# Stages of a hybrid decoder layer placed by a build-time clock of the engines' queues, with 32-row tiles for the sampled sequences

## The chip, the cores and the metric

The kernel runs on one core of one Trainium2 chip. The metric is the device time in microseconds of one execution of the whole program. A smaller number is better.

## What is computed

One decoder layer is applied to 1024 prompt tokens and to 8 sampled sequences of 8 new tokens each, 1088 tokens in all, with a model width of 1024:

```
x <- LN1(alpha*x + 0.5*SwiGLU_1(x))
x <- LN2(alpha*x + W_out[ attention group | HGRN2 group ](x))
x <- LN3(alpha*x + 0.5*SwiGLU_2(x))

attention: 8 heads of 64, 2 key/value heads, window 128, ALiBi, sinks
HGRN2, 4 heads, keys 128, values 128, per chunk of the sequence:
  b = cumsum(log f)
  o = (q*exp(b)) @ S + tril(sum_k q k exp(b_t - b_s)) @ v
  S = exp(b_last)*S + (k*exp(b_last - b))^T @ v
then rms norm of o, times silu(gate)
```

The prompt starts HGRN2 with S = 0. Each sampled sequence starts with a state of its own, S0, and its state after 8 tokens is an output. The feed-forward width is 2816, which is 22 blocks of 128 features.

## The kernel before

The whole layer is one straight program for five engines. TensorE multiplies, VectorE (DVE) and ScalarE (ACT) evaluate, GpSimd (POOL) helps, and SyncE (SP) issues the transfers. The order on each engine is the order in which the Python code emits instructions, and every engine runs its own list in that order. So an instruction whose operand is late holds up all that stands behind it on its engine.

Precision sets the form of the large products. A weight tile (`raw`) is split into a rounded part and a remainder (`hl`: one ACT cast, one DVE subtraction, in `hilo`), and so are the activations; each product is then three passes (`mmr`). The products inside attention and HGRN2 are single fp32 matmuls (`mm`), which the trace shows as two records each.

The stages of the program are, in order of time:

- **Gate and up of the first FFN** (0 to about 470 us): five feature blocks in plain form, the others with seven half-size products (`u`, `y`, `z`) from sums of operands. The results `go` are spilled to HBM as `gd`.
- **Down projection of the first FFN** (about 470 to 780 us): the tokens are cut into three groups `CH` of 512, 288 and 288 (ci 0, 1, 2). `g` features are read back and split (`g_item`). `trio(ci, ahead)` makes three output rows at once, feature by feature, with the first `ahead` features already there; `whole(m, cis, more)` makes one output row `m` and carries loads `more` for later units. When a group's last row is done, its layer norm `ln_T` starts: transposes `nat`, statistics, `rsqrt` on POOL, then `Y<-Y,rb` products on DVE.
- **Mixer** (about 780 to 1290 us): 22 projections of `W_in` (`pp`), and between their matmuls the attention blocks (`attn_block` 0 to 7), the sampled attention (`attn_sample`) and the HGRN2 heads (`hgrn` 0 to 3). Then `W_out` in two halves, `wout_a` from attention and `wout_b` from HGRN2 (`py`).
- **The second FFN** (about 1290 us to the end), like the first, with eight plain blocks, and with the last norm (`ln_out`, `ln_tail`) going out.

The work between the matmuls is written as Python generators, called sides. A side emits one stage and then yields a number of nanoseconds. `poll`, called after every group of large matmuls, runs the next stage of each side whose time has come. The clock for this is `s.t`, which counts planned TensorE time alone:

```python
def stage(s, d):
    lat = next(d.gen, "end")
    ...
        d.ready = s.t + (lat or 0.0)
```

So how far apart two stages stand is a constant in the code (`yield 1800.0` after each of the seven levels of `hgrn`, `yield 2500.0` behind an `rsqrt`), and the clock knows nothing of the queues of DVE, ACT, POOL or SP. Each fp32 matmul with its default `cols=1` is booked with at least 222 ns.

In `hgrn`, a level of the prompt multiplies 32-row tiles (`hgrn_b`, results to four 32-partition strips of one PSUM bank). The 64 sampled tokens have one 64-row product per level in a bank of their own (`hgrn_c`, and the second `hgrn_a`). Their output takes eight products with the states S0 (`hgrn_f`, 8 columns each), a copy `it`, and two products in `hgrn_g`. Their new states take two 512-column products (`hgrn_i`) over `Ve`, which spreads the values of 64 tokens over 8 sequences with the mask `em`.

Of the kernel before, what the change touches and what calls it, by code (L numbers as in the profile page):

```python
# [55 lines left out]
def const_arrays():  # L56
# [24 lines left out]
    em=np.zeros((64,8),np.float32)  # L81
    em[np.arange(64),np.arange(64)//8]=1
# [53 lines left out]
class Ker:  # L136
    def __init__(s, tc):
        s.tc = tc
        s.nc = tc.nc
# [46 lines left out]
    def pt(s, b):  # L186
        return s.pm.tile([P, 512], F32, tag="pm", name=s.nm(b))

    def st(s, b):
        return s.ps.tile([P, 512], F32, tag="ps", name=s.nm(b))  # L190

    def t2(s, b, w=512):
        return s.tmp.tile([P, 576], F32, tag="t2", name=s.nm(b))[:, :w]
# [4 lines left out]

    def mm(s, out, lhsT, rhs, start, stop, cols=1):
# [3 lines left out]
        s.nc.tensor.matmul(out, lhsT, rhs, start=start, stop=stop, skip_group_check=cols > 1)  # L203

    def mmr(s, out, lhsT, rhs, start, stop, loose=False):
        s.t += out.free_size() / 2.4 + 12.5
        s.nc.tensor.matmul(out, lhsT, rhs, start=start, stop=stop, skip_group_check=loose)  # L207

    def tr(s, out, in_, ident):
        s.t += 109.0  # L210
        s.nc.tensor.transpose(out, in_, ident)  # L211
# [12 lines left out]
    def add(s, gen, delay=0.0, rank=1):  # L224
        d = Side(gen, s.t + delay, rank)
        s.sides.append(d)
# [3 lines left out]
    def stage(s, d):  # L230
# [4 lines left out]
        else:  # L235
            d.ready = s.t + (lat or 0.0)

    def poll(s, most=3):
# [3 lines left out]
        for d in list(s.sides):  # L242
            if most and d.ready <= s.t:
# [7 lines left out]
    def until(s, true):  # L251
        while not true():
            r = [x for x in s.sides if x.ready <= s.t]
            if not r:
                s.t = min(x.ready for x in s.sides)
# [29 lines left out]
    def room(s, n):  # L285

        while s.live + n > NROWS:
# [5 lines left out]
            r = [x for x in s.sides if x.ready <= s.t] or [min(s.sides, key=lambda x: x.ready)]  # L293
            s.t = max(s.t, r[0].ready)
# [245 lines left out]
    def consts(s, a):  # L540
# [7 lines left out]
        s.em = s.cst.tile([64, 8], F32, name="em")  # L548
# [357 lines left out]
    def ffn_units(s, w13, w2, w2t, res, ln, nd, ready=None, tail=None):  # L906
# [269 lines left out]
        def whole(m, cis, more=(), bank=None, steps=None, drop=None, end=None):  # L1176
# [5 lines left out]
            for i, (j, nb) in enumerate(CUTS):  # L1182
                at.append(len(items))
                items.append(s.piece(w2t[m, :, j : j + nb], nb))
                k = -(-len(more) // (len(CUTS) - i))
# [37 lines left out]
        def norm(ci):  # L1223
            return lambda: s.lns.append(s.add(ln(ci), 500.0))
# [792 lines left out]
```

## Time and profile before

| what | value |
|---|---|
| median of 3 runs | 2102.89 us (2102.34 to 2106.88) |
| profiled execution | 2100.44 us |
| span, first to last instruction | 2098.7 us |
| granted TensorE clock, mean | 0.996 |
| TensorE busy | 2050.0 us, 98% |
| VectorE busy | 1214.9 us, 58% |
| ScalarE busy | 834.5 us, 40% |
| GpSimd busy | 178.3 us, 8% |

The profile is of one execution, and its times are those of that execution. A matmul's span reaches past the start of the next one, because matmuls are pipelined; so TensorE counts as idle only where it waits longer than that overlap. A group's busy time in the view by line is the time covered by its spans, so groups that alternate cover some of the same time. "Idle before" is the wait in front of a group and the instruction that ended it.

### The profile page before, as it was taken

The page shows a single profiled execution, that of the slowest core. Times are in us where ns is not written, and L with a number is a line of the kernel's source. Part 1 is how long each engine was busy: PE and PEld are TensorE (multiplying, and loading weights), DVE is VectorE, ACT ScalarE, POOL GpSimd, SP SyncE. Part 2 cuts the span into 40 slices and gives each one's busy share as a digit, 9 for nine tenths or more (in the row PEclk, how much of TensorE's full clock was granted, in tenths as well). Part 3 has the DMA queues.
Part 4 walks back from the last instruction along what each step waited for, and adds up shares of the span by engine and source line. Part 5 has one row for each costly group of instructions (what it writes and reads, how often), then busy time and mean ns, then how long its engine had stood idle before and what let it go on. Part 6 is the DMA issues. An engine that isn't in the chain of part 4 may idle for free.

```text
span 2098.7 us, 40231 instructions
## 1 busy us (share of the span) xinstructions
PE 2050.0 (98%) x16089; PEld 1933.8 (92%) x16089; DVE 1214.9 (58%) x2463; ACT 834.5 (40%) x1886; POOL 178.3 (8%) x353
## 2 busy tenths in 40 slices
PE   8999999999999999999999999999999999999998
PEld 8999999998899999878888888998999999888997
DVE  7766555555357552465644767576666655444855
ACT  5443333334336443444443233454343333432521
POOL 0000000000020210022213201300000000000121
PEclk9999999999999999999999999999999999999999
DMA  6332222227357331101111132342222222655832
GB/s 236 96 103 88 88 75 80 70 81 236 118 165 237 90 111 62 31 22 39 36 53 38 47 124 64 105 139 83 88 83 95 91 78 74 209 159 165 272 104 93
DMA packets 126124, 221.97 MB, mean 106 GB/s; under 512 B 14336, under 2 KB 44032, under 8 KB 125920
## 3 DMA queue, kind: packets, MB, share of 16 engines
q1 hardware_dynamic: 125936, 219.39, 33.0%
q8 instruction: 126, 2.06, 0.4%
q14 instruction: 62, 0.51, 0.1%
HBM read 181.69 MB, written 38.63 MB: 105 GB/s over the span
## 4 chain that ended last, share of the span: by engine, by line
PE 40%; DVE 6%; ACT 2%; issue 2%; DMA 1%; POOL 1%; DVEq 0%; SPq 0%; ACTq 0%; POOLq 0%
PE py L207 13%; PE u L207 7%; PE y L207 5%; PE pp L207 5%; PE pg L207 2%; PE pu L207 2%; DVE hl L409 2%; PE z L207 1%; ACT hl L408 1%; PE nat L211 1%; PE hgrn_b L203 1%; PE hgrn_e L203 0%; PE attn_block_c L203 0%; DMA raw<-in_w2tb 0%; ACT ev L918 0%
## 5 line engine op out<-in xcount | busy, mean ns | idle before, releaser
L207 PE MATMUL py<-g,hl 128*128 128x288 f32 (+3 forms) x3234 | 540.9, 327 | 6.8 <-DVE hl L409 4.6
L207 PEld LDWEIGHTS py<-g,hl 128*128 128x128 f32 x3234 | 487.4, 188 | 55.0 <-DVE hl L409 9.5
L409 DVE TENSOR_TENSOR hl<-raw,hl 128x512 fp32r<-128x512 f32 (+1 forms) x600 | 387.8, 659 | 224.4 <-ACT hl L408 222.5
L408 ACT CAST hl<-raw 128x512 fp32r<-128x512 f32 (+1 forms) x600 | 351.7, 593 | 404.9 <-PE py L207 187.0
L207 PE MATMUL u<-T,hl 128*128 128x288 f32 (+1 forms) x2700 | 365.3, 291 | 6.0 <-ACT ev L1049 5.0
L207 PEld LDWEIGHTS u<-T,hl 128*128 128x128 f32 x2700 | 349.9, 189 | 10.0 <-ACT ev L1049 7.9
L207 PE MATMUL pp<-Xh,hl 128*128 128x288 f32 (+1 forms) x1056 | 272.2, 335 | 0.0
L207 PEld LDWEIGHTS pp<-Xh,hl 128*128 128x128 f32 x1056 | 182.7, 189 | 19.9 <-issue 5.0
L207 PE MATMUL pp<-Xl,hl 128*128 128x288 f32 (+1 forms) x528 | 173.1, 328 | 0.0
L634 POOL TENSOR_SCALAR lnt<-lnr,lnp 128x1 f32<-128x1 f32 (+1 forms) x81 | 41.2, 508 | 1510.8 <-DVE lnr L630 843.0
L918 ACT ACTIVATE ev<-ev 128x288 f32<-128x288 f32 (+1 forms) x150 | 65.0, 434 | 258.3 <-DVE ev L1054 171.4
L207 PE MATMUL z<-B,hl 128*128 128x288 f32 (+1 forms) x900 | 121.8, 290 | 2.1 <-DVE ev L1054 2.1
L207 PE MATMUL y<-T,hl 128*128 128x288 f32 (+1 forms) x900 | 122.0, 290 | 0.6 <-DVE T L467 0.6
L207 PE MATMUL u<-B,hl 128*128 128x288 f32 (+1 forms) x900 | 121.7, 290 | 0.0
L207 PE MATMUL y<-B,hl 128*128 128x288 f32 (+1 forms) x900 | 121.7, 290 | 0.0
L207 PEld LDWEIGHTS z<-B,hl 128*128 128x128 f32 x900 | 117.0, 189 | 2.3 <-DVE ev L1054 2.3
L207 PEld LDWEIGHTS y<-T,hl 128*128 128x128 f32 x900 | 117.1, 189 | 0.8 <-DVE T L467 0.8
L207 PEld LDWEIGHTS y<-B,hl 128*128 128x128 f32 x900 | 117.0, 189 | 0.0
L207 PEld LDWEIGHTS u<-B,hl 128*128 128x128 f32 x900 | 117.0, 189 | 0.0
L207 PEld LDWEIGHTS pp<-Xl,hl 128*128 128x128 f32 x528 | 99.8, 189 | 6.2
L409 DVE TENSOR_TENSOR hl<-S,hl 128x512 fp32r<-128x512 f32 x88 | 60.9, 692 | 74.8 <-ACT hl L408 74.4
L207 PE MATMUL py<-oH,hl 128*128 128x288 f32 (+1 forms) x384 | 96.5, 332 | 1.4 <-DVE Y L1836 1.4
(273 smaller groups left out, 2404.8 us busy)
## 6 DMA issues: line engine op xcount, KB each, us to landing
raw<-in_w13b SPq DMA_DIRECT2D x120, 256.0 KB, 3.2
raw<-in_w13a SPq DMA_DIRECT2D x108, 256.0 KB, 3.2
raw<-in_w2ta SPq DMA_DIRECT2D x75, 256.0 KB, 3.6
raw<-in_w2tb SPq DMA_DIRECT2D x75, 256.0 KB, 3.5
gd<-go SPq DMA_DIRECT2D x44, 288.0 KB, 3.2
raw<-gd SPq DMA_DIRECT2D x88, 144.0 KB, 3.3
gd<-go SPq DMA_DIRECT2D x44, 256.0 KB, 3.5
raw<-gd SPq DMA_DIRECT2D x44, 256.0 KB, 4.5
```

The source lines that it names most:

```text
L203: s.nc.tensor.matmul(out, lhsT, rhs, start=start, stop=stop, skip_group_check=cols > 1)
L207: s.nc.tensor.matmul(out, lhsT, rhs, start=start, stop=stop, skip_group_check=loose)
L211: s.nc.tensor.transpose(out, in_, ident)
L408: lambda: nc.scalar.copy(hl[:, 0, :nb], src),
L409: lambda: nc.vector.tensor_tensor(hl[:, 1, :nb], src, hl[:, 0, :nb].bitcast(F32), ALU.subtract),
L634: e.tensor_scalar(t, r, r, hp, ALU.mult, ALU.mult)
L918: nc.scalar.activation(si, ps, AF.Silu)
```

## The change

The build now carries a clock of all queues. The four other engines are wrapped (`Watch`), and every instruction that is emitted is booked on its engine with a price from a table `COST`: it starts when its engine is free and its operands are written, plus 50 ns. Each tile remembers when it is written and last read. A DMA is booked on SP and on one bus. TensorE's clock `s.t` waits in the same way (`pe`).

A side may now yield tiles, and a count of PSUM banks, in place of a number. It is due when the clock says that these tiles are written, plus 100 ns, and that so many of the five `ps` banks come free. Most stages of `attn_block`, `attn_sample` and `hgrn` yield in that way. Matmuls in narrow tiles are booked with `cols=2` or `cols=4`, which changes their price in the clock and not the instruction.

For the sampled sequences in HGRN2, 64-row tiles become pairs of 32-row tiles in the banks of the prompt (`hgrn_a`, `hgrn_b`), and `hgrn_c` goes. `hgrn_f` and `it` go too: a block-diagonal copy of the queries, `qm`, goes straight against S0 in `hgrn_g`, which is now two strips of 32 rows with five products each. `hgrn_i` becomes eight products of 32 rows and 256 columns, into two banks in turn.

`trio(1, 12)` becomes `trio(1, 18)`: the last unit of group 0 carries ten features of group 1 where it carried four. The layer norms of groups 0 and 1 in both FFNs are "soft": `poll` passes them over while the clock has VectorE booked more than 800 ns ahead.

The rows below show three places, in the order in which the engine runs them. Lines L187, L334, L338 and L342 are the wrapper and the helpers `mm`, `mmr` and `tr` of the changed file.

First, TensorE in the mixer, at the transposes of attention block 0's output (`attn_block_e`) among the projections `pp`. Before:

```order
L207 MATMUL pp_9712<-Xh_7876,hl_9524 128x512
L211 MATMUL attn_block_e_9729<-ident,ao_9581 128x128 x4
L211 MATMUL attn_sample_c_9738<-ident,ss_9632 128x128
L211 MATMUL attn_sample_c_9738<-ident,ss_9632 64x128
L211 MATMUL attn_block_d_9745<-ident,as_9552 128x128 x4
L207 MATMUL pp_9712<-Xh_7877,hl_9577 128x512
```

And now:

```order
L338 MATMUL pp_9803<-Xh_8263,hl_9578 128x288
L342 MATMUL attn_block_e_9817<-ident,ao_9582 128x128 x4
L334 MATMUL attn_sample_a_9826<-cache_9178,sp_9789 32x64 x4
L334 MATMUL attn_sample_a_9826<-vs,sp_9789 32x64 x4
L342 MATMUL attn_block_d_9837<-ident,as_9549 128x128 x4
L334 MATMUL attn_block_c_9693<-vn_9114,pT_9797 128x64 x4
L338 MATMUL pp_9803<-Xh_8264,hl_9607 128x288
```

The block's transposes now come two half groups of projection matmuls later, and behind the sample's `attn_sample_c`, which they used to precede.

Second, TensorE at the sampled output of HGRN2 head 0, again among `pp`. Before, with the rows of two projection groups left out in the middle:

```order
L203 MATMUL hgrn_f_10910<-Q_9508,S_10799 128x8 x8
L207 MATMUL pp_10929<-Xh_7875,hl_10669 128x512
L207 MATMUL pp_10929<-Xl_7879,hl_10669 128x512
...
L207 MATMUL pp_10929<-Xh_7876,hl_10669 128x512
L203 MATMUL hgrn_g_10946<-Vs_9950,A_9968 64x128
L203 MATMUL hgrn_g_10946<-ident,it_10919 64x128
L207 MATMUL pp_10929<-Xh_7877,hl_10719 128x512
```

And now:

```order
L338 MATMUL pp_10740<-Xh_8264,hl_10389 128x288
L334 MATMUL hgrn_g_10790<-Vs_9950,A_9968 32x128 x2
L334 MATMUL hgrn_g_10790<-S_10718,qm 32x128 x8
L342 MATMUL attn_block_e_10805<-ident,ao_10590 128x128 x4
L338 MATMUL pp_10814<-Xh_8820,hl_10318 128x288
```

Two stages, of eight matmuls and of two, are now one stage of ten matmuls at one place in the list.

Third, VectorE in the first FFN's `trio` of group 1, while the norm of group 0 (`Y<-Y,rb`) is under way; `hl` of 384 columns is the weight remainder for one feature, `g` the split of a feature. Before:

```order
L409 TENSOR_TENSOR hl_6837<-raw_6658,hl_6837 128x384
L705 TENSOR_TENSOR Y_5825<-Y_5825,rb_6791 128x256
L706 TENSOR_TENSOR Y_5825<-Y_5825,rb_6791 128x256
L705 TENSOR_TENSOR Y_5825<-Y_5825,rb_6791 128x256
L706 TENSOR_TENSOR Y_5825<-Y_5825,rb_6791 128x256
L1117 TENSOR_TENSOR g_6851<-raw_6672,g_6851 128x288
L409 TENSOR_TENSOR hl_6853<-raw_6714,hl_6853 128x384
L1117 TENSOR_TENSOR g_6851<-raw_6728,g_6851 128x288
L409 TENSOR_TENSOR hl_6880<-raw_6773,hl_6880 128x384
```

And now:

```order
L187 TENSOR_TENSOR hl_6866<-raw_6687,hl_6866 128x384
L187 TENSOR_TENSOR Y_5827<-Y_5827,rb_6820 128x256 x4
L187 TENSOR_TENSOR hl_6880<-raw_6701,hl_6880 128x384
L187 TENSOR_TENSOR hl_6903<-raw_6743,hl_6903 128x384
L187 TENSOR_TENSOR Y_5828<-Y_5828,rb_6820 128x256 x4
L187 TENSOR_TENSOR hl_6917<-raw_6757,hl_6917 128x384
L187 TENSOR_TENSOR hl_6943<-raw_6802,hl_6943 128x384
```

Between two bursts of the norm there are now two weight tiles and no feature; the six features have moved into the unit before. The second half of that norm, four more bursts that used to follow within the next unit and a half, now comes two or three units later.

The diff, cut to what matters:

```diff
+class Clock:
+    HOP = 50.0
+    def there(s, ap):
+        lo, hi = s.span(ap)
+        return max((t for a, b, t in s.wrote.get(ap.name, ()) if a < hi and b > lo), default=0.0)
+    def soonest(s, tag, bufs, n=1):
+        q = s.tags.get(tag, [])
+        i = len(q) + n - 1 - bufs
+        return s.used.get(q[i], 0.0) if 0 <= i < len(q) else 0.0
+    def run(s, e, cost, outs, ins):
+        t = max([s.free[e]] + [s.there(x) + s.HOP for x in ins + outs]) + cost
+        s.free[e] = t
...
+COST = dict(
+    DVE=lambda op, n: 160.0 + 0.62 * n if op in ("tensor_scalar", "tensor_copy", "memset") else 150.0 + 1.05 * n,
+    ACT=lambda op, n: 195.0 + 0.78 * n,
+    POOL=lambda op, n: 100.0 + 0.85 * n if op == "memset" else 340.0 if n == 1 else 190.0 + 2.7 * n,
+)
...
+    def pe(s, out, lhsT, rhs, cost):
+        c = s.clock
+        t = max(s.t, c.there(lhsT) + c.HOP, c.there(rhs) + c.HOP, c.held.get(out.name, 0.0) + c.HOP)
+        s.wait(out, lhsT, rhs, t)
+        s.t = t + cost
...
     def mm(s, out, lhsT, rhs, start, stop, cols=1):
         n = out.free_size()
-        s.t += 2 * (max(111.0, n * (2 / 2.4) + 24.0) if cols == 1 else (n * (2 / 2.4) + 24.0) / cols)
+        s.pe(out, lhsT, rhs, 2 * (max(111.0, n * (2 / 2.4) + 24.0) if cols == 1 else (n * (2 / 2.4) + 24.0) / cols))
...
+    def due(s, d):
+        return max(d.ready, s.clock.soonest("ps", 5, d.banks) if d.banks else 0.0)
...
         for d in list(s.sides):
-            if most and d.ready <= s.t:
+            if most and s.due(d) <= s.t and not (d.soft and s.clock.free["DVE"] > s.t + 800.0):
...
-            return lambda: s.lns.append(s.add(ln(ci), 500.0))
+            return lambda: s.lns.append(s.add(ln(ci), 500.0, soft=ci < 2))
...
+            if last:
+                more = [g_items(1, *x) for x in ((8, 9), (9, 10), (10, 11), (11, 14), (14, 16), (16, 18))]
...
-        units.append(trio(1, 12))
+        units.append(trio(1, 18))
...  attn_block, behind the rsqrt and before the transposes
-        yield 2500.0
+        yield r
         nc.vector.tensor_scalar(o, o, r, None, ALU.mult)
-        yield 700.0
+        yield o, 1
...  hgrn, each level
-            if smp:
-                p2 = s.st("hgrn_c_")
-                s.mm(p2[:64, :32]..., KL[:, 1024:1088], v(QR[:, 1024:1088], 64, 1), True, True)
+            if smp:
+                for b in range(2):
+                    k0 = 1024 + 32 * b
+                    s.mm(ps[32 * b : 32 * b + 32, 128:144]..., KL[:, k0 : k0 + 32], v(QR[:, k0 : k0 + 32], 32, 1), True, True, cols=4)
...
-            yield 1800.0
+            yield KL, QR, 1
...  hgrn, sampled output
-        ps = s.st("hgrn_f_")
-        for b in range(8):
-            s.mm(ps[:, b * 8 : (b + 1) * 8], S0[:, b * P : (b + 1) * P], QR[:, 1024 + 8 * b : 1032 + 8 * b], True, True)
-        it = s.t2("it")
-        nc.scalar.copy(it[:, :64], ps[:, :64])
-        yield 500.0
+        nc.vector.tensor_copy(s.qm..., QR[:, 1024:1088]...)
+        yield s.qm, S0, 1
         ps = s.st("hgrn_g_")
-        s.mm(ps[:64, :P], A[:64, 1024:1088], Vs, True, False)
-        s.mm(ps[:64, :P], it[:, :64], s.ident, False, True)
+        for b in range(5):
+            for g in range(2):
+                out = ps[32 * g : 32 * g + 32, :P]
+                if b == 0:
+                    s.mm(out, A[:64, 1024 + 32 * g : 1056 + 32 * g], Vs, True, False, cols=2)
+                else:
+                    x = (4 * g + b - 1) * P
+                    s.mm(out, s.qm[:, g, 32 * b - 32 : 32 * b], S0[:, x : x + P], False, b == 4, cols=2)
...  hgrn, behind the rsqrt and before the transposes hgrn_h
-        yield 2800.0
+        yield r5
...
-        yield 2500.0
+        yield on, ons, 3
...  hgrn, new states
+        pss = [s.st("hgrn_i_") for q in range(2)]
+        for x in (slice(0, 256), slice(256, 512)):
+            for q in range(2):
+                r = slice(32 * q, 32 * q + 32)
+                s.mm(pss[q][:, x], Ks[r], Ve[r, x], True, True, cols=2)
         for q in range(2):
-            ps = s.st("hgrn_i_")
-            s.mm(ps, Ks, Ve[:64, q * 512 : (q + 1) * 512], True, True)
+            ps = pss[q]
```

More of the change, by code (lines that the diff above doesn't have):

```diff
@@ L92, with __init__, span, write @@
 NRAW = 7
+class Clock:
+    HOP = 50.0
+    def __init__(s):
+        s.free = dict(DVE=0.0, ACT=0.0, POOL=0.0, SP=0.0)
+        s.bus = 0.0
+        s.wrote = {}
+        s.used = {}
+        s.held = {}
+        s.tags = {}
+    @staticmethod
+    def span(ap):
+        p = ap.ap
+        st = abs(p[0][0])
+        if str(ap.space).endswith("DRAM"):
+            return ap.offset, ap.offset + sum(abs(a) * (b - 1) for a, b in p) + 1
+        o = ap.offset % st if st else ap.offset
+        return o, o + sum(abs(a) * (b - 1) for a, b in p[1:]) + 1
+    def there(s, ap):
+        lo, hi = s.span(ap)
+        return max((t for a, b, t in s.wrote.get(ap.name, ()) if a < hi and b > lo), default=0.0)
+    def write(s, ap, t):
+        lo, hi = s.span(ap)
+        s.wrote[ap.name] = [x for x in s.wrote.get(ap.name, ()) if x[0] < lo or x[1] > hi] + [(lo, hi, t)]
+        s.use(ap, t)
+    def use(s, ap, t):
+        s.used[ap.name] = max(s.used.get(ap.name, 0.0), t)
+    def fresh(s, ap, tag, bufs):
+        q = s.tags.setdefault(tag, [])
+        q.append(ap.name)
+        if len(q) > bufs:
+            t = s.used.get(q.pop(0), 0.0)
+            s.wrote[ap.name] = [(0, 1 << 30, t)]
+            s.held[ap.name] = t
+        return ap
+    def soonest(s, tag, bufs, n=1):
[5 more added lines that the diff above has]
+        s.free[e] = t
+        for x in ins:
+            s.use(x, t)
+        for x in outs:
+            s.write(x, t)
+        for x in ins + outs:
+            s.held[x.name] = t
+    def dma(s, out, in_):
+        t = max(s.free["SP"], s.there(in_) + s.HOP, s.there(out) + s.HOP) + 450.0
+        s.free["SP"] = t
+        n = 1
+        for a, b in out.ap:
+            n *= b
+        s.bus = max(s.bus, t + 800.0) + n * 4 / 330.0
+        s.use(in_, s.bus)
+        s.write(out, s.bus + 600.0)
@@ L95, with __init__ @@
+class Engines:
+    def __init__(s, clock, nc):
+        s.vector = Watch(clock, "DVE", nc.vector)
+        s.scalar = Watch(clock, "ACT", nc.scalar)
+        s.gpsimd = Watch(clock, "POOL", nc.gpsimd)
+        s.sync = Watch(clock, "SP", nc.sync)
+        s.tensor = nc.tensor
 class Side:
@@ L138, in __init__ @@
         s.tc = tc
-        s.nc = tc.nc
+        s.clock = Clock()
+        s.nc = Engines(s.clock, tc.nc)
         s.uid = 0
@@ L1513, in hgrn @@
         A = s.row(F32, "A")
-        yield 1000.0
-        nc.gpsimd.memset(A[:, :1024], 0.0)
-        D = s.mx.tile([P, 8, 32], F32, tag="D", name=s.nm("D"))
+        yield KL, QR, 1
+        nc.gpsimd.memset(A, 0.0)
+        D = s.mx.tile([P, 9, 32], F32, tag="D", name=s.nm("D"))
         ps = s.st("hgrn_a_")
```

177 lines of the change are left out of this document (116 added, 61 removed).

## The prediction

> **What bounds the kernel now.** I read the page first, for the busy shares, and then the table of stretches, since one share says nothing of where time can be had.
>
> ```profile
> span 2098.7 us, 40231 instructions
> PE 2050.0 (98%) x16089; PEld 1933.8 (92%) x16089; DVE 1214.9 (58%) x2463; ACT 834.5 (40%) x1886; POOL 178.3 (8%) x353
> ```
>
> TensorE (PE) is the bound, with 48.7 us idle in the whole span. So a change pays in two ways only: less TensorE work, or shorter waits of TensorE. Each row below is a stretch, its length, and the busy time of PE; the difference is TensorE's idle time.
>
> ```profile
> 600.00:700.00 100.00, 97.57 (x701) 93.71 (x700) 64.49 (x145) 50.02 (x107) 11.88 (x28) 1.00 0.60 186
> 850.00:1250.00 400.00, 387.45 (x4184) 338.08 (x4183) 239.60 (x569) 161.59 (x483) 89.02 (x148) 1.00 0.16 50
> 1290.00:1445.00 155.00, 145.25 (x1157) 142.55 (x1156) 113.73 (x221) 75.75 (x144) 16.78 (x42) 0.99 0.36 117
> 1925.00:1970.00 45.00, 41.26 (x297) 38.76 (x295) 38.72 (x86) 17.83 (x39) 11.99 (x24) 1.00 0.73 229
> 1970.00:2098.70 128.70, 117.67 (x905) 116.38 (x904) 71.27 (x144) 36.59 (x68) 19.91 (x37) 0.97 0.43 131
> ```
>
> That is 2.4 us at the first FFN's `trio` of group 1, 12.6 us in the mixer, 9.8 us at the second FFN's start, 3.7 us at its `trio`, and 11.0 us to the end. The granted clock is about 1.00 nearly everywhere, so nothing is to be had there. The view of TensorE's waits, taken by stretch (the first six rows are of the mixer), says who is late; its columns are the sum, the number and the longest.
>
> ```profile
> PE hgrn_b L203 <- POOL KL L1558: 3.1, 3, 1.9
> PE attn_block_e L211 <- DVE sden L1422: 1.8, 1, 1.8
> PE attn_sample_c L211 <- DVE ss L1425: 1.7, 1, 1.7
> PE hgrn_b L203 <- DVE Q L1557: 1.7, 2, 1.2
> PE attn_sample_d L203 <- ACT ssq L1463: 1.1, 1, 1.1
> PE nat_a L211 <- ACT V L1264: 1.1, 1, 1.1
> PE py L207 <- DVE hl L409: 1.9, 5, 0.7
> PE py L207 <- DVE hl L409: 2.1, 4, 1.0
> PE py L207 <- DVE g L1117: 1.5, 1, 1.5
> PE pg L207 <- ACT B L466: 2.7, 1, 2.7
> ```
>
> **Part 1, TensorE's work for the sampled sequences in HGRN2.** The view by line with shapes apart gives busy time and count of records, two for each emitted matmul:
>
> ```profile
> L203 PE MATMUL hgrn_f<-Q,S 128*128 128x8 f32 x64 | 7.4, 251 | 0.0
> L203 PE MATMUL hgrn_i<-KL,Ks 64*128 64x512 f32 x16 | 7.9, 615 | 0.0
> L203 PE MATMUL hgrn_g<-ident,it 128*64 128x128 f32 x8 | 1.7, 298 | 0.0
> L203 PE MATMUL hgrn_g<-Vs,A 64*64 64x128 f32 x8 | 1.7, 294 | 0.0
> L203 PE MATMUL hgrn_c<-Q,KL 128*64 128x32 f32 x24 | 3.6, 232 | 0.1
> L203 PE MATMUL hgrn_a<-Q,KL 128*64 128x64 f32 x8 | 1.3, 246 | 0.0
> L203 PE MATMUL hgrn_d<-Vn,F 128*128 128x128 f32 x64 | 8.5, 275 | 0.0
> L203 PE MATMUL attn_block_a<-kT,qT 64*128 64x256 f32 x56 | 16.0, 406 | 0.0
> L203 PE MATMUL hgrn_b<-Q,KL 128*32 128x16 f32 x1280 | 14.7, 185 | 4.8 <-POOL KL L1558 3.1 <-DVE Q L1557 1.7
> ```
>
> The first six rows go or change: 7.4 + 7.9 + 1.7 + 1.7 + 3.6 + 1.3 = 23.6 us. In their place come, for four heads: `hgrn_g` with 10 emitted matmuls of 128 columns each, 80 records in two column strips; `hgrn_i` with 4 of 256 columns, 32 records in two row strips; 24 more matmuls (48 records) in `hgrn_b` and 8 more (16 records) in `hgrn_a`. No row here shows these very tiles. If two strips run side by side, a pair costs what one record of a full tile does: 40 x 8.5/64 = 5.3 us for `hgrn_g`, and by the attention scores, whose row tiles a and b already run two at a time, 16 x 16.0/56 = 4.6 us for `hgrn_i`. The extra records cost, at the pace of `hgrn_b`, 64 x 14.7/1280 = 0.7 us. Sum 10.6 us, a saving of 13.0 us. If the strips run one after the other, it is 10.6 + 9.1 + 0.7 = 20.4 us, a saving of 3.2 us. I take 13.0: these pairs are nearest to two rows that overlap already. In `hgrn_b` four column strips start a record every 11.5 ns, though its mean record lasts 185 ns. The scores' row strips start together:
>
> ```profile
> 858.54 0.38 PE L203 MATMUL attn_block_a<-kT,qT 64*128 64x256 f32 x1
> 858.55 0.38 PE L203 MATMUL attn_block_b<-kT,qT 64*128 64x256 f32 x1
> 858.76 0.38 PE L203 MATMUL attn_block_a<-kT,qT 64*128 64x256 f32 x1
> ```
>
> A rule speaks against the column strips. The Trainium skill, "TensorE: Matmul & The Clock Gate", section "Part 3: Packing small matmuls — row/col tiling", says that a weight load runs under a matmul in flight only where the two use different row groups. By it `hgrn_g`, whose strips share all row groups, would gain nothing from pairing and cost 10.6 us, so that the saving would be 7.7 us. The pace of `hgrn_b`, whose strips share them too, does not bear that out.
>
> What else this part moves lies beside TensorE: per head one ACT copy (`it`) goes and two small ones come, one DVE copy (`qm`) comes, `Ve` on POOL halves. ACT is 40% busy in the mixer's stretch (161.59 of 400), DVE 60%, POOL 22%, so I cost that at nothing. The cover is that slack; gone, each late microsecond would show as a wait for A, `qm` or `Ve`.
>
> **Part 2, stages placed by the clock, in the mixer.** The waits behind a yield that now names its tiles are those of `hgrn_b`, `attn_block_e`, `attn_sample_c` and `attn_sample_d`: 3.1 + 1.7 + 1.8 + 1.7 + 1.1 = 9.4 us of the 12.6. The wait of `nat_a` and the rest stand outside it. An exact clock would remove 9.4 us; one that is no better than the constants would remove nothing. Two of its prices are low. It books the 13 small POOL instructions of a head's `rsqrt` at 13 x (190 + 2.7 x 9) = 2.8 us; the first and last of them in head 3, of 13 rows in the timeline, span 3.98 us:
>
> ```profile
> 1217.67 0.20 POOL L637 TENSOR_TENSOR hgt<-hgr 128x9 f32<-128x9 f32 x1 [6.27 <-DVE hgr L630]
> 1221.41 0.24 POOL L1652 TENSOR_SCALAR hr<-hgr 128x9 f32<-128x9 f32 x1
> ```
>
> So `hgrn_h`, which waits for nothing now, is placed 1.2 us early per head, 4.8 us for four. A stage can only stand between half groups of projections, which on average delays it by about as much, so I book half, 2.4 us. And it books VectorE's scaling of a block's output without regard to POOL:
>
> ```profile
> L1369 DVE TENSOR_SCALAR ao<-ao,atr x8: 478/483/1562, 874.5 to 1100.6; 128x512 f32<-128x512 f32 x8
> 874.40 0.95 POOL L1517 MEMSET A<- 128x1024 f32 x1
> 874.50 1.13 DVE L1369 TENSOR_SCALAR ao<-ao,atr 128x512 f32<-128x512 f32 x1
> 875.78 0.41 PE L211 MATMUL attn_block_e<-ident,ao 128*128 128x128 f32 x2 [1.85 <-DVE sden L1422]
> L1369 DVE TENSOR_SCALAR ao<-ao,atr 128x512 f32<-128x512 f32 x8 | 5.6, 698 | 4.5 <-POOL atr L635 4.5
> ```
>
> The minimum, median and maximum of eight are 478, 483 and 1562 ns; the 1.13 us one ran under a POOL memset, and TensorE stood 1.85 us behind it. The mean is 698 ns, so 8 x 0.215 = 1.7 us stays. The Trainium skill, "Advanced Engine Details and Errata", section "VectorE Performance Modes", says that VectorE's second SBUF port is shared with GpSimd and that the two block each other; the trace agrees. The part gives 9.4 - 2.4 - 1.7 = 5.3 us.
>
> **Part 3, ten features early and soft norms.** While group 0's norm runs, two features cost DVE one burst and two splits and two weight remainders:
>
> ```profile
> 644.37 0.41 DVE L705 TENSOR_TENSOR Y<-Y,rb 128x256 f32<-128x256 f32 x1
> 645.94 0.45 DVE L1117 TENSOR_TENSOR g<-raw,g 128x288 fp32r<-128x288 f32 x1
> 646.30 0.68 DVE L409 TENSOR_TENSOR hl<-raw,hl 128x512 fp32r<-128x512 f32 x1
> L207 PE MATMUL py<-g,hl 128*128 128x288 f32 x2046 | 285.4, 297 | 6.7 <-DVE hl L409 4.6 <-DVE g L1117 1.5
> ```
>
> From start to start a burst takes 1.57 us and a split 0.36; a 384-column remainder lies between that and the 0.60 of 512 columns, say 0.5. That is 1.57 + 0.72 + 1.0 = 3.3 us, against 18 matmuls of 285.4/2046 us, 2.5 us, on TensorE. DVE falls behind by 0.8 us per burst. Without the two splits it needs 2.6 us and keeps up. The features go to a unit of 512-column matmuls, and the late half of the norm to units behind; over the whole 600 to 700 stretch DVE is 64% busy, which is the cover. Moving six `gd` reads ahead leaves SP's number of transfers as it is. The two stretches hold 2.4 + 3.7 = 6.2 us idle; I take three quarters, 4.6, since DVE is 86% busy in the second (38.72 of 45) and the norm's work stays. If the soft norm slips too far, what is late next is group 1's input of the first projection.
>
> **Part 4, nothing.** The start of the second FFN (9.8 us, with 2.7 of it for `B`) keeps its order of norm, sums and plain blocks, and the tail (11.0 us) its own. No gain, no loss; either could be 2 us.
>
> **The sum.** 13.0 + 5.3 + 4.6 = 22.9 us off the profiled execution's 2100.4 us gives 2077.5 us. That execution stands 2.5 us under the median of its runs, 2102.9; so 2080 us.
>
> **Rivals.**
> - *The waits only change places* (2090). For it: TensorE waits 48.7 us of 2098.7 already, every stage moved, and the prices above are low. Against: the present constants ignore the queues. Then part 1 alone stays, 2102.9 - 13.0 = 2090.
> - *The strips run in turn* (2090). Part 1 gives 3.2, the others 9.9: 2102.9 - 13.1 = 2090. By the skill's rule alone, 7.7 + 9.9 off, 2085. Against both stands `hgrn_b`'s pace.
> - *The clock runs ahead of the chip, and TensorE waits at each stage* (slower). The clock books a pair of scores at 2 x 2 x (256 x 2/2.4 + 24) = 0.95 us; the rows at 858 us show 0.21 per pair of records, so 0.42. A score stage of two pairs puts the clock 1.06 us ahead, and what is placed next comes too early by up to that. Six places in each of eight blocks, 48, could pay it. It decides at 13.0 + 4.6 + 12.6 = 30 us, 28 places; at all 48, 50.9 us, the time is 2102.9 - 30.2 + 50.9 = 2124. Against: work placed well behind a score is due by later writes, which move with the clock.
> - *No change that can be measured*: 20 such places take back 21 of the 22.9 us, 2101.
>
> **How the numbers follow.** The forecast has a chance of 0.57, its own range 2070 to 2087. The waits changing places has 0.15, the strips in turn 0.11 (0.03 of it by the skill's rule), no change 0.09, slower 0.08. 0.2% is 4.2 us, about what a measurement of this kernel can tell from no change. Faster is 0.57 + 0.15 + 0.11 = 0.83. The low end takes 13.0, all of 12.6 and of 6.2, and 2 at the second FFN: 33.8 off, 2069; I go to 2067. The high end takes in the two rivals at 2090 and some new waits, 2096.
>
> **What would show it.** Right: `hgrn_f` and `hgrn_c` gone, `hgrn_g` near 5 us, `hgrn_i` near 5; under 8 us idle in the mixer, no waits of `py` for `hl` over 1 us at the `trio`. Wrong: `hgrn_g` near 11, new waits in front of `hgrn_h` or `attn_block_d`, or a gap at group 1's first projection.

## The result, and the profile after

The changed kernel takes 2075.0 us (median of four executions, 2073.2 to 2076.4) against 2104.3 (2102.3 to 2106.9): a ratio of 0.9862, interval 0.9849 to 0.9874, 29 us less. The forecast was 2080 us, its own range 2070 to 2087. The profiled execution took 2073.2 us, 27.2 less than that of before. The page's first lines:

```profile
span 2071.5 us, 40371 instructions
PE 2029.2 (98%) x16137; PEld 1922.3 (93%) x16137; DVE 1213.9 (59%) x2467; ACT 834.2 (40%) x1890; POOL 180.9 (9%) x354
```

TensorE's busy time fell by 20.8 us and its idle time by 6.4, to 42.3. The groups of HGRN2's sampled tiles, by line with shapes apart:

```profile
L334 PE MATMUL hgrn_b<-Q,KL 128*32 128x16 f32 x1328 | 15.1, 185 | 2.2 <-POOL KL L187 1.9 <-DVE Q L187 0.3
L334 PE MATMUL hgrn_i<-KL,Ks 32*128 32x256 f32 x32 | 4.5, 400 | 0.0
L334 PE MATMUL hgrn_g<-S,qm 128*32 128x128 f32 x64 | 4.3, 276 | 0.0
L334 PE MATMUL hgrn_g<-Vs,A 64*32 64x128 f32 x16 | 1.6, 281 | 0.0
```

`hgrn_f` and `hgrn_c` are gone; 5.9 + 4.5 us and half a microsecond of extra records stand where 23.6 stood, 12.7 us less. From the view of TensorE's waits over the whole span, rows that bear on the prediction (sum, number, longest):

```profile
PE pg L338 <- ACT B L187: 8.5, 2, 5.8
PE py L338 <- DVE hl L187: 3.9, 6, 1.5
PE pu L338 <- ACT si L187: 2.2, 1, 2.2
PE hgrn_b L334 <- POOL KL L187: 1.9, 2, 1.2
PE attn_block_b L334 <- ACT sp L187: 0.9, 1, 0.9
```

The waits of `attn_block_e`, `attn_sample_c` and `attn_sample_d` are gone, nothing waits in front of `hgrn_h`; the wait of `pu` for `si`, at 24.6 us, is new. To see where the time went I cut both traces at the same instructions (the first `trio` matmul, the first attention score, the first `w_out` matmul and so on) and compare the stretches. Each row is start and end, length, TensorE's busy time, then its clock and two columns on DMA. By such cuts the stages of the kernel before begin at 485.7 us (down projection), 761.6 (mixer) and 1300.1 (second FFN), some 10 to 20 us off the round times of the list of stages. First the three of before, then of after: group 1's `trio` and the rest of the down projection, attention and HGRN2, and the same as the first for the second FFN.

```profile
608.00:761.60 153.60, 151.17 (x1127) 1.00 0.54 162
835.20:1178.10 342.90, 334.29 (x3729) 1.00 0.12 39
1926.90:2074.90 148.00, 143.69 (x1072) 1.00 0.57 176
```

```profile
609.20:758.50 149.30, 148.90 (x1127) 1.00 0.53 162
832.10:1157.50 325.40, 322.71 (x3773) 1.00 0.13 41
1902.10:2047.70 145.60, 141.71 (x1072) 1.00 0.55 173
```

The mixer's stretch is 17.5 us shorter, the two `trio` stretches 4.3 and 2.4. Of the rest, from the same cuts: -3.3 from `w_out` to the second FFN, -1.0 at that FFN's start, +1.2 in all that lies ahead of the first `trio`, the tail the same. From 850 to 1250 us TensorE is now idle for 6.3 us instead of 12.6.

### The profile page after: what moved, and what is told of

It reads as the page before. It is cut to its first block, busy times and chain, and to the rows that moved or that the text cites. A ratio compares the mean times of both kernels' runs of the same rounds, so it can differ in the third digit from the quotient of the medians.

```text
span 2071.5 us, 40371 instructions
## 1 busy us (share of the span) xinstructions
PE 2029.2 (98%) x16137; PEld 1922.3 (93%) x16137; DVE 1213.9 (59%) x2467; ACT 834.2 (40%) x1890; POOL 180.9 (9%) x354
## 4 chain that ended last, share of the span: by engine, by line
PE 40%; DVE 6%; DMA 2%; ACT 2%; issue 1%; POOL 0%; DVEq 0%; SPq 0%; ACTq 0%; POOLq 0%
PE py L338 13%; PE u L338 7%; PE y L338 5%; PE pp L338 5%; PE pu L338 2%; PE pg L338 2%; DVE hl L187 2%; PE z L338 1%; ACT hl L187 1%; DMA raw<-in_w2tb 1%; DVE ev L187 1%; DVE Y L187 1%; DVE S L187 1%; ACT ev L187 1%; PE nat L342 1%
## 5 line engine op out<-in xcount | busy, mean ns | idle before, releaser
L338 PE MATMUL py<-g,hl 128*128 128x288 f32 (+3 forms) x3234 | 536.7, 326 | 4.4 <-DVE hl L187 3.9
L338 PEld LDWEIGHTS py<-g,hl 128*128 128x128 f32 x3234 | 486.9, 188 | 48.8 <-DVE hl L187 5.5
L187 DVE TENSOR_TENSOR hl<-raw,hl 128x512 fp32r<-128x512 f32 (+1 forms) x600 | 392.4, 667 | 227.1 <-ACT hl L187 225.0
L187 ACT CAST hl<-raw 128x512 fp32r<-128x512 f32 (+1 forms) x600 | 351.3, 592 | 394.3 <-PE py L338 153.6
L338 PE MATMUL u<-T,hl 128*128 128x288 f32 (+1 forms) x2700 | 365.2, 291 | 5.9 <-ACT ev L187 5.9
L338 PEld LDWEIGHTS u<-T,hl 128*128 128x128 f32 x2700 | 349.9, 189 | 9.8 <-ACT ev L187 9.0
L338 PE MATMUL pp<-Xh,hl 128*128 128x288 f32 (+1 forms) x1056 | 271.3, 334 | 0.0
L338 PEld LDWEIGHTS pp<-Xh,hl 128*128 128x128 f32 x1056 | 182.0, 188 | 18.7 <-issue 4.2
L187 POOL TENSOR_SCALAR lnt<-lnr,lnp 128x1 f32<-128x1 f32 (+1 forms) x81 | 44.2, 545 | 1499.9 <-DVE lnr L187 833.9
L338 PE MATMUL pp<-Xl,hl 128*128 128x288 f32 (+1 forms) x528 | 172.5, 327 | 0.0
L187 ACT ACTIVATE ev<-ev 128x288 f32<-128x288 f32 (+1 forms) x150 | 65.0, 434 | 257.9 <-DVE ev L187 257.9
L338 PE MATMUL z<-B,hl 128*128 128x288 f32 (+1 forms) x900 | 121.8, 290 | 2.1 <-DVE ev L187 2.1
L338 PE MATMUL y<-T,hl 128*128 128x288 f32 (+1 forms) x900 | 122.0, 290 | 0.6 <-DVE T L187 0.6
L338 PE MATMUL y<-B,hl 128*128 128x288 f32 (+1 forms) x900 | 121.7, 290 | 0.0
L338 PE MATMUL u<-B,hl 128*128 128x288 f32 (+1 forms) x900 | 121.7, 290 | 0.0
L338 PEld LDWEIGHTS z<-B,hl 128*128 128x128 f32 x900 | 117.0, 189 | 2.3 <-DVE ev L187 2.3
L338 PEld LDWEIGHTS y<-T,hl 128*128 128x128 f32 x900 | 117.1, 189 | 0.8 <-DVE T L187 0.8
L338 PEld LDWEIGHTS y<-B,hl 128*128 128x128 f32 x900 | 117.0, 189 | 0.0
L338 PEld LDWEIGHTS u<-B,hl 128*128 128x128 f32 x900 | 117.0, 189 | 0.0
L187 ACT COPY ev<-u 128x288 f32<-128x288 f32 (+1 forms) x225 | 86.1, 382 | 58.8 <-PE u L338 57.7
L187 DVE TENSOR_TENSOR ev<-y,ev 128x288 f32<-128x288 f32 (+1 forms) x150 | 66.2, 441 | 71.0 <-PE y L338 40.6
L338 PEld LDWEIGHTS pp<-Xl,hl 128*128 128x128 f32 x528 | 99.4, 188 | 6.0
```

What stands on the lines that cost most here:

```text
L187: r = f(*a, **k)
```

## The experiments

All ratios are to the kernel before. 0.001 is 2.1 us; an interval is about +-2.7 us wide, so the difference of two kernels is good to some 4 us.

| kernel | median us | ratio (95%) | less than before, us |
|---|---|---|---|
| the change | 2075.0 | 0.9862 (0.9849-0.9874) | 29.0 |
| small tiles alone | 2094.4 | 0.9962 (0.9950-0.9974) | 8.0 |
| clock alone | 2094.6 | 0.9964 (0.9950-0.9977) | 7.6 |
| change without part 3 | 2084.8 | 0.9911 (0.9899-0.9924) | 18.7 |
| change without the tiles | 2089.2 | 0.9927 (0.9914-0.9939) | 15.4 |
| change, norms not soft | 2077.4 | 0.9874 (0.9861-0.9887) | 26.5 |
| change, features late | 2083.7 | 0.9907 (0.9893-0.9922) | 19.6 |
| change, strips in turn | 2080.7 | 0.9892 (0.9879-0.9905) | 22.7 |
| change, constant delays | 2104.1 | 1.0000 (0.9992-1.0009) | 0.0 |
| change, prices halved | 2107.7 | 1.0022 (1.0013-1.0032) | -4.6 |
| change, prices up 30% | 2091.0 | 0.9939 (0.9928-0.9951) | 12.8 |
| change, fitted prices | 2078.2 | 0.9876 (0.9861-0.9890) | 26.1 |
| change, a wait filled | 2076.1 | 0.9865 (0.9852-0.9878) | 28.4 |

### The parts one by one

The small tiles put into the kernel before: `hgrn` is that of the change, with the constants of before in its yields:

```diff
-        yield KL, QR, 1
+        yield 4000.0
...
-        yield s.qm, S0, 1
+        yield 500.0
```

> The kernel before with HGRN2's small tiles alone; constant delays, no clock, features and norms as before. Theory (the parts add up): the tiles are worth the 12.7 us by which the busy time of their groups fell in the changed kernel, so 2104.3 - 12.7 = 2091.6 us, with the mixer's waits of before still there (hgrn_b for KL and Q, attn_block_e, attn_sample_c: about 9 us together). Rival A (the tiles pay only with the clock: TensorE gets through a head sooner and then stands before the same late KL, so the time comes back as waits): 2098 to 2104 us, with hgrn_b's waits up from 4.8 to 10 us or more. Rival B (the freed hgrn_c banks shorten waits too): 2086 us or less.

8.0 us: between the theory and rival A. The mixer's stretch in this kernel, and two of its waits there:

```profile
835.50:1171.40 335.90, 323.88 (x3773) 1.00 0.12 40
PE attn_block_e L211 <- DVE ao L1372: 1.7, 1, 1.7
PE hgrn_b L203 <- DVE F L1568: 1.6, 2, 0.9
```

TensorE works 10.4 us less there than before, but the stretch is only 7.0 shorter, as its idle time rises from 8.6 to 12.0 us; both waits shown are new. Next the clock with the tiles and without part 3, which is the change less these lines:

```diff
-            return lambda: s.lns.append(s.add(ln(ci), 500.0, soft=ci < 2))
+            return lambda: s.lns.append(s.add(ln(ci), 500.0))
...
-                more = [g_items(1, *x) for x in ((8, 9), (9, 10), (10, 11), (11, 14), (14, 16), (16, 18))]
...
-        units.append(trio(1, 18))
+        units.append(trio(1, 12))
```

> The changed kernel with the features back in the unit behind (12 early instead of 18, spread as before) and the norms not soft. Theory (part 3 is worth what the two trio stretches lost, 4.3 + 2.4 us): 2081.7 us, py waits for hl of 1 us and more at group 1's trio again. Rival A (the stretches gain by the clock's placing of the norms' stages, which is kept here): 2075 to 2077 us. Rival B (without them the stretches are worse than before, because the norm comes at another time): 2085 us or more.

It is 10.3 us slower than the change, which is rival B's number; the theory's 6.7 is not excluded by it. Its stretches, in the order of those above:

```profile
609.30:763.20 153.90, 151.11 (x1126) 1.00 0.55 162
836.90:1162.50 325.60, 322.64 (x3773) 1.00 0.13 41
1908.00:2058.70 150.70, 143.87 (x1072) 1.00 0.56 173
```

The mixer is that of the change (325.6 against 325.4) and 10.3 us shorter than with the tiles alone, 9.1 of it idle time (12.0 to 3.0): that is the clock. The two `trio` stretches are 4.6 and 5.1 us longer than in the change: that is part 3. The second varies between executions, so I took means: in the four kernels without part 3 (before, tiles alone, clock alone and this one) the stretches last 153.7 and 149.4 us, in four with it (the change, without the tiles, strips in turn, a wait filled) 149.6 and 146.2, which makes 4.1 + 3.2 = 7.3 us. Rival B's reason is not borne out: undone, the stretches are about those of the other kernels without part 3. Part 3's two halves were undone singly, with the first line of that diff and with the others:

> The changed kernel with the norms not soft (a norm's stage is placed when its operands are there, whatever VectorE's queue); the features stay early. With both halves of part 3 undone the two trio stretches were 4.6 and 5.05 us longer. Theory (the features early carry most of it, since they take the splits and remainders out of the norm's way): 2 to 3 us slower than the changed kernel, 2077 to 2078 us, with py's waits for hl at group 1's trio under 1 us. Rival A (softness carries it, and features early without it only fill VectorE sooner): 2082 us or more, both stretches long again. Rival B (either alone is enough): 2075 us.

> The changed kernel with the features spread as before (12 early, eight of them in the units ahead, six left to the units behind); the norms stay soft. Theory (the features carry most): 2081 to 2083 us, both trio stretches 3 to 4 us longer. Rival A (softness carries it): 2076 to 2078 us. Rival B (either alone is enough): 2075 us.

Without softness it is 2.5 us slower, as the theory says, but within the 4 us that two kernels can differ by chance; the stretches are 1.4 and 0.5 us above the means with part 3. With the features late it is 9.4 us slower, a little more than the theory's 6 to 8, and not spread as it said: +1.8 at the first `trio`, +5.9 at the second. There one wait is longer than any with both halves undone (1.8 us at most):

```profile
1961.75 2.35 PE L338 MATMUL py<-g,hl 128*128 128x288 f32 x12 [4.15 <-DVE hl L187]
```

By this row of the timeline TensorE stands 4.15 us for one weight remainder, which VectorE makes behind a stage of a norm (1956.9 to 1960.3 us). Features late with soft norms (0.9907) is not measurably better than both undone (0.9911). So the early features are shown to matter; that softness gains anything is not. Now the tiles taken out of the change, and the clock alone, without tiles and part 3:

> The changed kernel with HGRN2's sampled tiles of before (hgrn_f, hgrn_c, 64-row hgrn_i and hgrn_a) under the clock, stages named by their tiles. Put on the kernel before by themselves the small tiles gave 8 to 9 us of the 12.7 by which their groups' busy time fell, and TensorE's idle time rose by 5. Theory (the constants let 4 us of that slip back as waits, a clock that follows the queues does not): undone here they cost the whole 12.7, 2087 to 2089 us, with the mixer's waits no longer than in the changed kernel. Rival A (the small tiles are worth 8 to 9 here too): 2083 to 2084 us. Rival B (under the clock longer TensorE work covers more of the other engines' work): 2081 us or less.

> The kernel before with the clock and the named stages alone: HGRN2's tiles of before, features and norms as before. The clock on top of the small tiles (from those alone to the changed kernel without part 3) was worth 10.7 us by the ratios; the small tiles alone 8.0, and under the clock 13.7. Theory (the parts lean on each other: tiles alone leave 5 us to new waits, which the clock then takes): the clock alone is worth 18.7 - 13.7 = 5 us, the size that the prediction gave it, 2098 to 2099 us. Rival A (the clock is worth its 10.7 us by itself, and the tiles' gain under it is smaller than measured): 2093 us. Rival B (part 3 carries more without the tiles, the clock alone nothing): 2102 to 2104 us.

Without the tiles 13.6 us are lost, as the theory says; the mixer's stretch is idle for 4.5 us there, against 2.7, where the theory had no more. The clock alone gave 7.6, between the theory's 5 and rival A's 10.7, and with its interval excludes neither; only rival B falls. So the tiles are worth 8.0 alone, 11.1 under the clock and 13.6 in the whole change, the clock 7.6 alone and 10.7 on the tiles. From the first attention score to the second FFN the profiled executions are 9.0 us shorter with the tiles alone, 8.3 with the clock alone and 20.6 with both. That the parts help each other is read from these lengths and from the idle times (8.6 before, 12.0 with the tiles, 3.0 with tiles and clock), one execution each, not from the ratios, whose intervals overlap.

### The strips

```diff
-        for b in range(5):
-            for g in range(2):
+        for g in range(2):
+            for b in range(5):
...
-        for x in (slice(0, 256), slice(256, 512)):
-            for q in range(2):
+        for q in range(2):
+            for x in (slice(0, 256), slice(256, 512)):
```

> The changed kernel, with the matmuls of hgrn_g written strip after strip (five of one strip, then five of the other) and those of hgrn_i likewise; the same instructions. Theory (the strips gain by running side by side): in turn the 80 records of hgrn_g take 80 x 8.5/64 = 10.6 us instead of 5.9, and the 32 of hgrn_i 9.1 instead of 4.5; 2075.0 + 4.7 + 4.6 = 2084 us. Rival A (column strips that share row groups never run side by side, and hgrn_g's 5.9 us come from the tiles' smaller size): hgrn_g stays near 5.9, hgrn_i goes to 9, 2079.6 us. Rival B (the order of writing does not matter, TensorE's queue finds the other strip by itself): both stay, 2075 us.

6.3 us slower. One head's `hgrn_g` in the timeline, first of the change, then in turn:

```profile
949.35 0.41 PE L334 MATMUL hgrn_g<-Vs,A 64*32 64x128 f32 x4
949.69 1.07 PE L334 MATMUL hgrn_g<-S,qm 128*32 128x128 f32 x16
950.76 0.44 PE L342 MATMUL attn_block_e<-ident,ao 128*128 128x128 f32 x2
```

```profile
950.77 0.40 PE L334 MATMUL hgrn_g<-Vs,A 64*32 64x128 f32 x2
951.11 1.06 PE L334 MATMUL hgrn_g<-S,qm 128*32 128x128 f32 x8
952.10 0.40 PE L334 MATMUL hgrn_g<-Vs,A 64*32 64x128 f32 x2
952.43 1.06 PE L334 MATMUL hgrn_g<-S,qm 128*32 128x128 f32 x8
953.42 0.44 PE L342 MATMUL attn_block_e<-ident,ao 128*128 128x128 f32 x2
```

The same 20 records take 1.41 us alternating and 2.65 in turn; over four heads the two groups go from 5.9 to 11.7 us, which is 5.8 of the 6.3. By line with shapes apart, in turn:

```profile
L334 PE MATMUL hgrn_g<-S,qm 128*32 128x128 f32 x64 | 8.5, 276 | 0.0
L334 PE MATMUL hgrn_g<-Vs,A 64*32 64x128 f32 x16 | 3.2, 281 | 0.0
L334 PE MATMUL hgrn_i<-KL,Ks 32*128 32x256 f32 x32 | 4.6, 400 | 0.0
```

`hgrn_i` did not change: 4.5 us in the change, 4.6 in turn. So the theory holds for the column strips and fails for the row strips, and rival A is the reverse of what happened. The Trainium skill, "TensorE: Matmul & The Clock Gate", "Part 3: Packing small matmuls — row/col tiling", lets a weight load run under a matmul only where the two use different row groups. The two strips of `hgrn_g` share all of theirs, and 70 ns per record against 132 does not agree with the prediction's reading of it, that they would gain nothing. Whether it is the loads or the matmuls that overlap, these rows do not tell.

### The prices of the clock

The constants of before in `attn_block`, `attn_sample` and `hgrn`, all else as changed:

```diff
-        yield r
+        yield 2500.0
         nc.vector.tensor_scalar(o, o, r, None, ALU.mult)
...
```

> The changed kernel with the constant delays of before back in attn_block, attn_sample and hgrn; the clock goes on pricing TensorE's own waits, and tiles, features and soft norms stay. Theory (the named yields remove the mixer's waits): the waits of hgrn_b, attn_block_e, attn_sample_c and attn_sample_d come back, 6 to 9 us together, 2081 to 2084 us. Rival A (what removed them is the clock's view of TensorE's own time, or the shorter tiles, and not the named yields): 2075 to 2077 us. Rival B (the constants no longer fit a clock that books the small tiles at a quarter): 2090 us or more, with waits that the kernel before does not have.

Rival B, and further than it said: the constants cost 29 us, all that the change gave. The mixer's stretch is 27.2 us longer than in the change, 17.1 of it idle; the other 10.1 are the same work at a lower granted clock (0.97 in the mean). This row and the longest groups of TensorE's waits in it:

```profile
835.20:1187.80 352.60, 332.80 (x3774) 0.97 0.12 38
PE attn_block_e L342 <- DVE ao L187: 12.3, 3, 4.5
PE attn_sample_c L342 <- DVE ss L187: 3.9, 3, 1.8
```

One of the three, in the timelines of POOL, DVE and PE:

```profile
940.41 0.29 POOL L187 TENSOR_TENSOR sat<-sar 128x64 f32<-128x64 f32 x1 [3.46 <-DVE atp L187]
945.33 0.32 POOL L187 TENSOR_TENSOR sar<-sar,sat 128x64 f32<-128x64 f32 x1
945.64 0.38 POOL L187 TENSOR_SCALAR att<-atr,atp 128x1 f32<-128x1 f32 x1
948.03 0.29 POOL L187 TENSOR_SCALAR atr<-att,atr 128x1 f32<-128x1 f32 x1
948.36 1.25 DVE L187 TENSOR_SCALAR ao<-ao,atr 128x512 f32<-128x512 f32 x1 [1.80 <-POOL atr L187]
949.76 1.09 PE L342 MATMUL attn_block_e<-ident,ao 128*128 128x128 f32 x4 [4.43 <-DVE ao L187]
```

The sampled sequences' `rsqrt` (12 instructions, 940.4 to 945.6) stands ahead of the block's in POOL's queue, and a constant of 2500 ns cannot know that. These constants were set for the old clock, which books the small tiles higher. So the run shows what they cost under the new clock, not what constants set anew would; how much of the loss comes from the lower bookings, rival B's reason, is not separated. Then all prices of DVE, ACT and POOL scaled, by 0.5 and by 1.3:

```diff
-        t = max([s.free[e]] + [s.there(x) + s.HOP for x in ins + outs]) + cost
+        t = max([s.free[e]] + [s.there(x) + s.HOP for x in ins + outs]) + 0.5 * cost
```

> The changed kernel with every price of VectorE, ScalarE and GpSimd in the clock halved; TensorE's and the transfers' prices stay. So stages are placed too early. Theory (it is the size of the prices that takes the mixer's waits away): waits in front of attn_block_e, hgrn_b and attn_sample_c come back, 10 us or more together, some of them over 2 us with a lower granted clock behind them; 2090 us or more. Rival (the order of the queues is what matters, the sizes little): 2075 to 2080 us.

> The changed kernel with every price of VectorE, ScalarE and GpSimd in the clock 30% higher. So stages are placed later. Theory (too late costs nothing as long as plain projections stand between): the mixer's remaining waits (hgrn_b for KL 1.9, attn_block_b 0.9) go or stay under 3 us, the time within 3 us of the changed kernel's, 2072 to 2078 us. Rival (late stages leave the heads' chain without cover at the mixer's end, or hold banks longer): new waits behind 1150 us and 2080 us or more.

Halved they cost 33.6 us, with 26.0 us idle in the mixer's stretch (358.1 long, with some work in it that the change does later); the theory holds. At 1.3 times the theory fails: it costs 16.2 us. The rival's place, the mixer's end, has 5.4 of it (from `w_out` on), with new waits of 2.3 us for `oL` and 2.5 in front of `hgrn_h`; the attention's stretch is only 1.9 longer, but the first projection 7.1 (3.0 of it idle, at a granted clock of 0.96) and the second `trio` 4.6.

```profile
797.04 0.40 PE L338 MATMUL pp<-Xh,hl 128*128 128x288 f32 x1 [1.48 <-ACT Xh L187]
800.60 0.61 PE L338 MATMUL pp<-Xl,hl 128*128 128x288 f32 x1 [1.18 <-DVE Xl L187]
```

These waits, in the first projection, are those of group 1's input: the norm comes too late. A norm is soft by the clock's view of VectorE's queue, which is now too long; that this is what held it back is argued, not shown. Last, prices nearer to the trace of the change (its VectorE and ScalarE rows run some 50 and 100 ns above the price for each operand of one number per partition; a ScalarE instruction of 128x256, priced at 395 ns, takes 498 with one and 597 with two):

```diff
+            if max(x.free_size() for x in outs) > 1:
+                cost += {"DVE": 50.0, "ACT": 100.0, "POOL": 0.0}[s.name] * sum(x.free_size() == 1 for x in ins)
...
-340.0 if n == 1 else 190.0 + 2.7 * n
+430.0 if n == 1 else 306.0 if n < 64 else 190.0 + 2.5 * n
```

> The changed kernel with prices nearer to the durations in its trace: 50 ns more on VectorE and 100 ns on ScalarE for each operand that is one number per partition, 55 ns for copy_predicated, GpSimd 430 ns at one element, 306 ns at nine and 2.5 ns an element above, and the score matmuls at half. Prices halved cost 33 us and prices 30% up 16 us. Theory (the prices are near their best already, what is left in the mixer are 5 us of waits): 2072 to 2077 us, hgrn_b's 1.9 us wait for KL gone or moved. Rival A (a nearer price places every stage better): 2070 us or less. Rival B (the planner is touchy: any other set of prices gives another placing with waits of its own, the shown one being picked out of many): 2080 us or more.

2.9 us slower by the ratios, just outside the theory's range; neither rival. The 1.9 us for `KL` went, a wait of 1.9 for `Q` came. Whether the loss comes from the placing or is chance stays open.

A part of these losses is the granted clock. Taken in steps of 2 us, the sum of (1 - clock) x 2 us up to 2060 us is 0.0 us in the profile of the change, 3.4 in that of before, 15.4 with the constants, 15.3 at half the prices, 12.0 at 1.3 times and 6.8 with the fitted ones, in dips of 1.7 or 3.4 us, most of them behind waits. So of the 35 and 39 us by which the profiles with the constants and with halved prices are longer than that of the change, up to 15 are the clock, of the 17 with prices up it is up to 12, and the 7 of the fitted prices can all be clock.

### A wait filled

```diff
+        if out.name.endswith("_14751") and start:
...
+                for _ in range(9):
+                    s.nc.tensor.matmul(out[:, :P], s.ident, s.ident, start=True, stop=True, skip_group_check=True)
```

> The changed kernel with nine matmuls of 128 columns, 2.4 us of work that nobody uses, put into TensorE's 2.70 us wait for B at the second FFN's start. In six of the ten profiles so far the granted clock was half for some 3.4 us behind this wait, which costs 1.7 us; in the others it was not. Theory (the wait itself brings the clock down): no stretch below 1.0 behind it, the first pg group's 12 matmuls there 1.6 us; 2073 to 2074 us, 1 us less than the changed kernel on the mean. Rival A (the dips come at times of their own): they stay. Rival B (the filler delays B's matmuls): 2076 us or more.

What it is about: behind the 2.70 us wait at the second FFN's start most profiles show TensorE at half its clock. Here the kernel with the strips in turn, as stretches of 5 us (length, busy, number, clock) and in the timeline, and then the filled one:

```profile
1290.00:1295.00 5.00, 2.15 (x12) 0.80 0.95 356
1295.00:1300.00 5.00, 5.00 (x26) 0.52 0.28 116
1293.42 3.44 PE L338 MATMUL pg<-B,hl 128*128 128x256 f32 x12 [2.70 <-ACT B L187]
```

```profile
1285.00:1290.00 5.00, 3.97 (x33) 1.00 0.93 362
1288.30 0.38 PE L344 MATMUL pg<-B,hl 128*128 128x256 f32 x1 [0.69 <-ACT B L188]
1290.00:1295.00 5.00, 4.57 (x40) 1.00 0.28 111
```

26 records in 5 us of work there, 40 in 4.57 us here. Of the 13 profiles with the wait unfilled, counting before and the change, ten have the dip (not those of the change, of features late and of prices up 30%; of the ten taken when the expectation was written it was seven, not six). Filled, there is none here or anywhere else ahead of 2060 us, all four executions have a mean clock of 0.998 (the change 0.995 to 0.998), and their times spread over 1.0 us instead of 3.2. The time itself, 2076.1 us, is the same as the change's within the interval. One profile without the dip says little, since three of 13 have none; the four mean clocks say more. So it is likely, though not proved, that the wait brings the dip, as the theory says; that filling it saves time is not shown.

## Why the prediction came out as it did

**The time.** 2075.0 lies in the range and in the forecast's own; 5 us below the forecast. In the order tiles, clock, part 3 the gain is 8.0 + 10.7 + 10.3 us by the ratios; forecast were 13.0 + 5.3 + 4.6. So the total is closer than its terms: part 1 was 5 us too high, part 2 and part 3 more than 5 too low, and that these errors partly cancel is luck.

**Part 1, 13.0.** The working was right: the rows fell by 12.7, `hgrn_g` took 5.9 (5.3 foretold) and `hgrn_i` 4.5 (4.6). `hgrn_g` is cheap because its strips alternate, as was said; for `hgrn_i` that reason is wrong. What the step passed over is the sentence "I cost that at nothing": sooner TensorE work uncovers other engines, 3.4 us of new idle time with the constants. Under the clock that is not so, and the step holds (13.6).

**Part 2, 5.3.** Too small with the tiles in; for the clock alone, 7.6 by the ratios, it is within the noise. Both deductions failed. The 2.4 us for `hgrn_h`, placed early by POOL's low price: nothing waits there. The 1.7 us for VectorE's scaling of `ao` that POOL slows: the change still has a run of 1295 ns (minimum, median and maximum in the row), but no wait of `attn_block_e`.

```profile
L187 DVE TENSOR_SCALAR ao<-ao,atr x8: 474/478/1295, 877.0 to 1095.5; 128x512 f32<-128x512 f32 x8
```

With neither, 9.4 us of waits behind changed yields would have been the term; the clock took 9.1 us of idle time from the mixer's stretch once the tiles were in. That this is so near to 9.4 is partly chance, since 3.4 of it are waits that the tiles alone had brought.

**Part 3, 4.6.** Mis-sized: 7.3 us by the stretches, 10.3 by the ratios. The step that failed is "The two stretches hold 2.4 + 3.7 = 6.2 us idle", used as a bound. Idle time shows only a part of a wait. The records of the 288-column matmuls, here and in the change without part 3, by line with shapes apart:

```profile
L338 PE MATMUL py<-g,hl 128*128 128x288 f32 x2046 | 281.2, 296 | 4.3 <-DVE hl L187 3.9 <-ACT hl L187 0.4
L338 PE MATMUL py<-g,hl 128*128 128x288 f32 x2046 | 285.5, 297 | 9.6 <-DVE hl L187 5.4 <-ACT hl L187 1.8 <-DVE g L187 1.8
```

The same 2046 records are 4.3 us "busier" where more waits. A record of this size lasts 0.29 us while the next may start 0.13 us behind it (28 of them take 3.89 us in the kernel before, at 757.8 us), so a wait of up to 0.16 us is counted as busy. Group 1's first `trio` stretch had 2.4 us of idle time, lost 2.0 of it and still became 4.3 us shorter. The mechanism was right for the features, which cost 9.4 us when late; for the softness, 2.5 us, it is not shown.

**Part 4, nothing.** -1.0 us at the second FFN's start and 0.0 at the tail: within the 2 us that were allowed. The +1.2 us ahead of the first `trio`, which the prediction does not name, go with the new wait of `pu` for `si` (2.2 us); the two kernels without the clock do not have it.

**The clock.** "Nothing is to be had there" was wrong for the profiled execution of before. Windows of 100 us hide this:

```profile
920.00:925.00 5.00, 3.31 (x15) 0.79 0.00 0
925.00:930.00 5.00, 5.00 (x102) 0.87 0.02 3
1310.00:1315.00 5.00, 3.96 (x19) 0.70 0.78 318
```

Two dips, behind the 1.69 us wait of `attn_sample_c` and the 2.70 us one of `pg`, cost up to (0.21 + 0.13 + 0.30 + 0.05) x 5 = 3.4 us (0.05 is from the 5 us behind the third row); the profiled execution of the change has none ahead of 2060 us. Its other executions do have lower mean clocks: 0.9965 over all four, against 0.9947 over 53 executions of before that stand beside the experiments, where a straight line gives 1.0 us for each 0.001. So some 2 us of the medians' 29 is clock by this estimate.

**The rivals.** That the waits only change places was true of the tiles alone, in part (3.4 us of 10.4), and not under the clock. The strips in turn give 6 us back, measured, where the rival took 10. That the clock runs ahead of the chip is a real danger: at half the prices the change is 4.6 us slower than before. At the prices as they are it doesn't: the score stages, booked at twice their time, show no waits but 0.9 us at `attn_block_b`. Of the signs named, `py` still waits for `hl` over 1 us at the second `trio` (1.5 and 1.2), and under 8 us idle in the mixer came true with 6.3.

## What to carry to other kernels

Size a stall by cutting two traces at the same instructions and comparing lengths: idle time leaves out whatever part of a wait the pipelined records cover, and here that was half. Where a planner places work by prices, the prices count as much as the planner: half of them cost 34 us, more than the 29 gained, 1.3 times of them 16, and constants set for another clock all 29. Part of such a loss is the granted clock behind the new waits. A nearer set of prices gained nothing. Write matmuls in column strips alternating, not strip by strip.

## What was not expected of the hardware

- TensorE's clock falls to half behind waits of under 3 us. Behind 2.70 us in ten of 13 profiles, behind the 2.1 us wait of `z` in four of 14, behind 1.69 us in the kernel before, and behind each of the five waits of 3.1 to 4.6 us that the runs have; once, without the tiles, behind 0.62 us (at 952 us). A dip takes up to 1.7 us (0.79 and 0.87 over 5 us each) or 3.4 (the one shown with the strips in turn). What decides whether a wait is followed by one was not found. The Trainium skill, "TensorE: Matmul & The Clock Gate", "Part 1: The HAM clock gate", puts the fall behind an idle window of about 3.4 us; in these rows it follows shorter waits too.
- Two strips of 32 rows gain nothing by alternating: 32 records of `hgrn_i` take 4.5 us either way, where 16 of 64 rows and twice the columns took 7.9. What makes them cheap was not isolated.
